# A kernel for a two-layer decoder trunk: in the second layer the weights' low part is made by ScalarE and an accumulating DMA instead of VectorE

## The chip, the core and the metric

The kernel runs on one core of one Trainium2 chip. TensorE (PE in the profile) multiplies and transposes, VectorE (DVE), ScalarE (ACT) and GpSimd (POOL) work on tiles in the on-chip memory, and SyncE (SP) issues the transfers from the device's memory. Every engine works through its own list of instructions in order; semaphores hold an instruction back until what it reads is there. The metric is the device time of one execution in microseconds (us), the median of several runs; lower is better.

## What is computed

The input is 512 positions of 1024 features in float32, the output has the same shape. There are two layers, each `x <- LayerNorm(alpha * x + sublayer(x))`.

The first (even) layer has two head groups, retention and a recurrent branch, which share one input projection and one output projection. The second (odd) layer is differential attention:

```
proj = einsum('bsd,de->bse', x, w_in);  q, k, v, g = split(proj)
q = rope(q) * d**-0.5;  k = rope(k)                        # 16 maps of 128 features
s = where(causal, q @ k^T, -inf);  p = softmax(s)          # two maps a head
w = p[:, :, 0] - lam * p[:, :, 1];  out = w @ v            # 8 heads of 256 features
out = out * rsqrt(mean(out**2) + eps) * subln_g * (1 - lambda_init) * silu(g)
y = out @ w_out
```

The input projection of the second layer is a 1024 x 8192 matrix, its output projection a 2048 x 1024 one. Everything is float32.

## The kernel before, in words

**Products.** To keep float32 precision, each operand is kept as two tiles of the matmul's own float32 format: a high part `h`, which is the value rounded by a cast, and a low part `l`, which is the value minus the high part. `mm3` (L148 to L151) adds three products for each product wanted: high by high, high by low, low by high.

**Weights.** A weight matrix comes in pieces of 128 x 1024 (512 KB). `order` lists them in the order of use: pieces 0 to 63 belong to the first layer, 64 to 143 to the second. 64 of the second layer's 80 pieces come from its input projection (`in_od_w`, no scale); the other 16 come from its output projection (`in_od_wo`) and are scaled while they are split. `fetch` (L163) takes the next piece: SP loads it into one of two raw buffers `w_r` (L171), and `split` (L139) makes the two parts: ScalarE casts `w_r` into `w<n>h` (L145), then VectorE writes `w_r` minus `w<n>h` into `w<n>l` (L146). A piece with a scale goes by L142 and L143. There are five buffers for split pieces (`wsp`), so the cast of piece n waits until TensorE has used piece n-5. For pieces 64 and 65, two further buffers are there (`wx`).

**Units of work.** The input projection is done in units. A `t_unit` takes one piece and gives 128 rows of q or k for all positions; an `s_unit` takes four pieces and gives v or g for four blocks of 128 positions (`sb`); an `out_unit` takes four pieces of the output projection. `take(ahead)` hands out the next piece and has written the fetches of `ahead` further pieces by then. Since TensorE's and SP's instructions stand in program order, this says where the loads stand on SP; the order on the other three engines comes from a list scheduler, which places an instruction by its own estimate of when everything is ready, with the priorities that the code gives (`tc.high_priority`).

**The order on TensorE** is written out: between the products of a unit, `side.tick()` starts steps of the other work (heads of attention, transposes after the LayerNorm) at counted places.

**From the first layer to the second.** The last `out_unit` of the first layer (`eo`) gives for each `sb` two banks of sums. VectorE adds them to `y` (L239), takes statistics (L334, L336), and normalises in two steps: L340, and after GpSimd has made the reciprocal root `lrs` (L325, L326) L342. TensorE transposes the result (`ht`, L561), ScalarE and VectorE split it into `hh` and `hl`. Then the first `s_unit` (`ov0`, pieces 64 to 67) starts.

**One block of attention** (a head, 128 positions; 32 blocks): TensorE scores `as`, VectorE the row minimum (L591), ScalarE the exponentials `e` (L594), VectorE the difference of the two maps (L602), TensorE transposes (`wt`, L606), ScalarE and VectorE split, TensorE multiplies by v into the bank `po`, of which there is one. Then ScalarE sums squares (L621), GpSimd makes the reciprocal root `ars` (`rs_t` L325, `ars` L326), VectorE multiplies (`o`, L625), TensorE transposes `o` back into `po` (L630), ScalarE and VectorE split it into `om<hd>h` and `om<hd>l`. Only then can the next block use the bank.

Of the kernel before, what the change touches and what calls it, by code (L numbers as in the profile page):

```python
# [8 lines left out]
F32 = mybir.dt.float32  # L9
F32R = mybir.dt.float32r  # L10
AF = mybir.ActivationFunctionType
ALU = mybir.AluOpType
# [83 lines left out]
def trunk(ctx: ExitStack, tc: tile.TileContext, a):  # L96
    nc = tc.nc
# [21 lines left out]
    ALL = slice(None)  # L119
# [7 lines left out]
    def bank(pl, tag, name):  # L127
        return pl.tile([P, 512], F32, tag=tag, name=name)

    def pair(pl, shape, tag, name, **kw):  # L130
        return tuple(pl.tile(shape, F32R, tag=tag + x, name=name + x, **kw) for x in "hl")
# [4 lines left out]
    def cut(t, *ix):  # L136
        return t[0][ix], t[1][ix]

    def split(src, dst, scale=None):  # L139
        if scale is not None:  # L140
            s = sg[:, scale:scale + 1]
            nc.scalar.activation(out=dst[0], in_=src, func=AF.Identity, scale=s)  # L142
            nc.vector.scalar_tensor_tensor(out=dst[1], in0=src, scalar=s, in1=dst[0].bitcast(F32), op0=ALU.mult, op1=ALU.subtract)  # L143
            return
        nc.scalar.copy(out=dst[0], in_=src)  # L145
        nc.vector.tensor_tensor(out=dst[1], in0=src, in1=dst[0].bitcast(F32), op=ALU.subtract)  # L146

    def mm3(out, l, r, start, stop):  # L148
        nc.tensor.matmul(out=out, lhsT=l[0], rhs=r[0], start=start, stop=False)  # L149
        nc.tensor.matmul(out=out, lhsT=l[0], rhs=r[1], start=False, stop=False)  # L150
        nc.tensor.matmul(out=out, lhsT=l[1], rhs=r[0], start=False, stop=stop)  # L151

    def load(name, shape, src, pl=None, tag=None, bufs=None):
        t = (pl or const).tile(shape, F32, tag=tag or name, name=name, bufs=bufs)
        nc.sync.dma_start(out=t, in_=src)
        return t
# [3 lines left out]
    order, ready = [], []  # L160
    extra, stats = {}, {}

    def fetch(parts=((0, D),)):  # L163
        if len(ready) < len(order):
            n = len(ready)
            src, scale = order[n]
            raw = wraw.tile([P, D], F32, tag="raw", name=f"w{n}_r")
            w = pair(extra.pop(n, wsp), [P, D], "w", f"w{n}")
            for lo, hi in parts:
                c = slice(lo, hi)  # L170
                nc.sync.dma_start(out=raw[:, c], in_=src[:, c])  # L171
                split(raw[:, c], cut(w, ALL, c), scale=scale)
                yield
            ready.append(w)

    taken = [0]

    def take(ahead):
        taken[0] += 1
        while len(ready) < min(taken[0] + ahead, len(order)):  # L180
            list(fetch())
        return ready[taken[0] - 1]

    def t_unit(act, name):
        w = take(2)
        ps = bank(ps_pj, "pj", name + "_ps")
        for kt in range(KT):
            mm3(ps, cut(w, ALL, slice(kt * P, kt * P + P)), cut(act, ALL, kt), kt == 0, kt == KT - 1)
            side.tick()
        return ps  # L190
# [65 lines left out]
    for kind, i in ev:  # L256
        if kind in ("ro", "lo", "out"):
            order += [(eo[2 * i + j + n], None) for n in {"ro": (0,), "lo": (8,), "out": (8, 0)}[kind] for j in range(2)]
        else:
            n = 4 if kind == "v" else 1  # L260
            order += [(ew[ei + j], None) for j in range(n)]
            ei += n
    order += [(eo[n], None) for n in (14, 15, 6, 7)]
    od = [("v", 0), ("g", 0), ("qk", 0), ("qk", 1), ("qk", 2)]
    for g in range(1, 4):
        od += [("g", g), ("v", g), *[("o", (2 * g - 2, 2 * g - 1))] * (g < 3), ("qk", 2 * g + 1), *[("qk", 2 * g + 2)] * (g < 3)]
# [20 lines left out]
    x = pair(big, [P, KT, S], "x", "x")  # L287
    xr = big.tile([P, KT, S], F32, tag="y", name="xr")
    halves = fetch(((0, HALF), (HALF, D)))
    for n, (lo, hi) in enumerate(((0, 1), (1, 2), (2, 4), (4, 6), (6, 8))):  # L290
        nc.sync.dma_start(out=xr[:, lo:hi], in_=a["xt"][:, lo:hi])
        for kt in range(lo, hi):
            split(xr[:, kt], cut(x, ALL, kt))
        if n < 2:
            next(halves)
            if n == 1:
                list(halves)
        elif n < 4:
            list(fetch())
# [217 lines left out]
    for kind, i in ev:  # L517
        if kind == "v":
            if i:
                for j in range(4):  # L520
                    side.need(job["ret", j], lambda: j in seen)
            v = v_even(i)
        elif kind == "xb":
            if i % 2 == 0:
                raw = load(f"gw{i}", [P, 4 * P], a["gw"][i // 2], pl=es, tag="es")
                gw[0] = pair(two, [P, 4 * P], "gw", f"gw{i}", bufs=1)
                split(raw, gw[0])
            job["lru", i] = side.add(lru(i, t_unit(x, f"xb{i}"), mixes(("lru", i // 2))), "lru", 2)
        elif kind == "q":
            dec[i] = load(f"dec{i}", [P, S], a["dec"][i], pl=two, tag="dec")  # L530
            q[i] = rope(t_unit(x, f"q{i}"), "q", f"q{i}")
        elif kind == "k":
            job["ret", i] = side.add(retention(i, q.pop(i), rope(t_unit(x, f"k{i}"), "k", f"k{i}"), v, dec.pop(i), mixes(("ret", i // 2))), "ret", 1, RET_START[i])
        elif kind in ("ro", "lo", "out"):
            even_out({"ro": ("ret",), "lo": ("lru",), "out": ("lru", "ret")}[kind], i, f"{kind}{i}")
        else:
            ps = t_unit(x, f"{kind}{i}")
            if len(users) >= 5:
                side.need(job[users[-5]])
            users.append(("ret" if kind == "gr" else "lru", i))  # L540
            g = gp.tile([P, S], F32, tag="g", name=f"{kind}{i}")
            silu(ps, g, f"{kind}{i}")
            gates[kind, i] = g
        if (kind, i) == ("gr", 1):
            for sb in range(SB):
                nc.sync.dma_start(out=y[:, sb], in_=a["x"][sb])
# [227 lines left out]
```

## Time and profile before

| | |
|---|---|
| median of 3 runs | 944.74 us (944.48 to 944.75) |
| the profiled execution | 944.8 us, its span in the profile 943.0 us |
| busy share of the span | PE 98%, DVE 73%, ACT 49%, POOL 6% |
| granted TensorE clock | 0.997 |
| transfers | 88.94 MB, 94 GB/s over the span, all issued by SP |
| the second layer's matmuls | begin at 409.6 us |

How to read it: a row of the timeline gives the start in us from the span's start, the duration in us, the engine, the line of the kernel, the operation, `out<-in` by the program's names, and in brackets the engine's idle time before it and what released it. Buffer numbers are left out in most names, but pieces and heads keep theirs (`w85h` is the high part of piece 85). The names `w00h` to `w73h` with two digits that stand beside `po` are not pieces but the transposed attention weights of a head and block. Matmuls overlap: their durations are longer than the distance between their starts, so starts are what counts.

### The profile page before, as it was taken

To read this page: it belongs to the slowest core of one execution; us is meant where nothing else is said; L and a number is where in the kernel's file an instruction comes from. 1 tells how busy PE (TensorE), PEld (TensorE's weight loads), DVE (VectorE), ACT (ScalarE), POOL (GpSimd) and SP (SyncE) were. 2 spreads that over 40 slices of the span, in tenths; PEclk is the share of its full clock that TensorE was granted. 3 is DMA by queue.
4 is the path that set the end of the run, shared out by engine and by line. 5 is a ranking of instruction groups with operands and counts; after the bars stand their busy time and mean duration, and the time that the engine had idled before them with its cause. 6 is when DMAs were issued, how large, how long until landed. Compare 5 with 4: busy or idle time off the path is not lost.

```text
span 943.0 us, 11558 instructions
## 1 busy us (share of the span) xinstructions
PE 924.9 (98%) x4327; PEld 764.4 (81%) x4327; DVE 692.8 (73%) x1171; ACT 462.7 (49%) x749; POOL 55.7 (6%) x117
## 2 busy tenths in 40 slices
PE   9999999999999999999999999999999999999995
PEld 7888888878887888888887888888788888887884
DVE  5877997878779988994489854478744488536687
ACT  5567786566474776423334454233453234444230
POOL 0000000000000000000001210100100001101012
PEclk9999999999999999999999999999999999999998
DMA  6562221512314123314221222042222142223102
GB/s 224 169 222 68 86 75 53 167 57 93 120 52 149 57 90 119 119 27 164 96 88 63 70 88 90 23 134 90 68 72 85 48 132 67 87 79 116 55 23 90
DMA packets 27416, 88.94 MB, mean 94 GB/s; under 512 B 3424, under 2 KB 3552, under 8 KB 27360
## 3 DMA queue, kind: packets, MB, share of 16 engines
q1 hardware_dynamic: 27360, 88.20, 28.1%
q8 instruction: 34, 0.56, 0.2%
q14 instruction: 22, 0.18, 0.1%
HBM read 86.09 MB, written 2.10 MB: 94 GB/s over the span
## 4 chain that ended last, share of the span: by engine, by line
PE 73%; DVE 13%; ACT 5%; issue 4%; DMA 2%; POOL 2%; SPq 0%; POOLq 0%; DVEq 0%; ACTq 0%
PE ov_ps L149 3%; PE ov_ps L150 3%; PE ov_ps L151 3%; PE og_ps L149 3%; PE og_ps L150 3%; PE og_ps L151 3%; PE oo_ps L149 2%; PE oo_ps L150 2%; PE oo_ps L151 2%; DMA w_r<-in_ev_w 2%; PE xb_ps L151 1%; PE xb_ps L149 1%; PE xb_ps L150 1%; PE gl_ps L149 1%; PE gl_ps L151 1%
## 5 line engine op out<-in xcount | busy, mean ns | idle before, releaser
L594 ACT ACTIVATE e<-as,nm 128x128 f32<-128x128 f32 (+3 forms) x64 | 33.2, 523 | 29.2 <-DVE nm L591 28.8
L625 DVE SCALAR_TENSOR_TENSOR o<-po,ars,og 128x256 f32<-128x256 f32 x32 | 15.5, 483 | 40.0 <-POOL ars L326 40.0
L591 DVE CUSTOM_DVE_ANT_0 as<-as,mask 128x128 f32<-128x128 f32 (+3 forms) x64 | 30.1, 509 | 1.9 <-PE as L151 1.9
L601 POOL TENSOR_SCALAR zr<-z 128x1 f32<-128x1 f32 x32 | 11.3, 352 | 308.9 <-ACT e L594 308.9
L325 POOL TENSOR_SCALAR rs_t<-bmv 128x1 f32<-128x1 f32 x8 | 3.8, 470 | 429.2 <-DVE bmv L336 429.2
L621 ACT ACTIVATE po<-po 128x256 f32<-128x256 f32 x32 | 11.9, 371 | 29.9 <-PE po L151 29.8
L325 POOL TENSOR_SCALAR rs_t<-ss,zr 128x1 f32<-128x1 f32 x32 | 15.9, 496 | 140.8 <-ACT po L621 135.8
L239 DVE TENSOR_TENSOR y<-oo_ps,y 128x512 f32<-128x512 f32 x24 | 16.2, 683 | 4.2 <-PE oo_ps L151 4.2
L326 POOL TENSOR_TENSOR ars<-rs_t,nhalf 128x1 f32<-128x1 f32 x32 | 18.9, 590 | 2.7
L466 DVE SCALAR_TENSOR_TENSOR xc<-xbp,vecs,xc 128x509 f32<-128x509 f32 (+2 forms) x24 | 17.8, 743 | 1.5 <-ACT xc L463 1.3
L602 DVE SCALAR_TENSOR_TENSOR e<-e,zr,e 128x128 f32<-128x128 f32 (+3 forms) x32 | 17.6, 551 | 1.0
L599 DVE RECIPROCAL zr<-z 128x1 f32<-128x1 f32 x32 | 5.2, 162 | 15.1 <-ACT e L594 14.9
L423 DVE TENSOR_TENSOR rsd<-rs,dec 128x512 f32<-128x512 f32 (+3 forms) x32 | 15.4, 483 | 0.9 <-PE rs L151 0.7
L630 PEld LDWEIGHTS po<-ident,o 128*128 128x128 f32 x64 | 8.3, 140 | 7.7 <-DVE o L625 4.5
L630 PE MATMUL po<-ident,o 128*128 128x128 f32 x64 | 12.6, 278 | 1.4 <-DVE o L625 1.3
L606 PE MATMUL wt<-ident,e 128*128 128x128 f32 x80 | 14.0, 273 | 0.0
L606 PEld LDWEIGHTS wt<-ident,e 128*128 128x128 f32 x80 | 10.4, 140 | 3.9 <-DVE e L602 0.4
L145 ACT CAST hh<-ht 128x512 fp32r<-128x512 f32 x8 | 4.7, 588 | 17.4 <-PE ht L561 17.4
L482 DVE TENSOR_TENSOR xbp<-xbp,xc 128x512 f32<-128x512 f32 x8 | 5.5, 690 | 10.0 <-ACT xbp L479 10.0
L594 ACT ACTIVATION_READ_ACCUMULATOR e<-as,nm 128x1 f32 x64 | 12.5, 196 | 0.0
L488 DVE SCALAR_TENSOR_TENSOR xc<-t,r 128x512 f32<-128x512 f32 x8 | 5.5, 691 | 9.0 <-ACT r L487 9.0
L342 DVE SCALAR_TENSOR_TENSOR y<-y,lrs,ln 128x512 f32<-128x512 f32 x16 | 11.3, 746 | 0.9 <-POOL lrs L326 0.9
(2665 smaller groups left out, 3411.2 us busy)
## 6 DMA issues: line engine op xcount, KB each, us to landing
w_r<-in_od_w SPq DMA_DIRECT2D x64, 512.0 KB, 3.3
w_r<-in_ev_w SPq DMA_DIRECT2D x47, 512.0 KB, 3.3
w_r<-in_ev_wo SPq DMA_DIRECT2D x16, 512.0 KB, 3.4
w_r<-in_od_wo SPq DMA_DIRECT2D x16, 512.0 KB, 3.3
dec<-in_dec SPq DMA_DIRECT2D x8, 256.0 KB, 3.8
y<-in_x SPq DMA_DIRECT2D x4, 512.0 KB, 6.8
out_h<-y SPq DMA_DIRECT2D x8, 256.0 KB, 2.1
xr<-in_xt SPq DMA_DIRECT2D x3, 512.0 KB, 7.1
```

The lines of the kernel that those rows point to most:

```text
L149: nc.tensor.matmul(out=out, lhsT=l[0], rhs=r[0], start=start, stop=False)
L150: nc.tensor.matmul(out=out, lhsT=l[0], rhs=r[1], start=False, stop=False)
L151: nc.tensor.matmul(out=out, lhsT=l[1], rhs=r[0], start=False, stop=stop)
L239: nc.vector.tensor_tensor(out=yy, in0=ps, in1=yy, op=ALU.add)
L325: nc.gpsimd.tensor_scalar(out=t, in0=var, scalar1=scale, scalar2=eps, op0=ALU.mult, op1=ALU.add)
L326: nc.gpsimd.tensor_tensor(out=out, in0=t, in1=nhalf[:, :1], op=ALU.pow)
L466: nc.vector.scalar_tensor_tensor(out=xc[:, sh:], in0=xb[:, :S - sh], scalar=conv_w(w, c), in1=xc[:, sh:], op0=ALU.mult, op1=ALU.add)
L591: nc.vector.tensor_tensor_reduce(out=ps[:, :n], in0=ps[:, :n], in1=mask[:, S - n:], scale=-QK_SCALE, scalar=3.0e38, op0=ALU.add, op1=ALU.m ...
L594: nc.scalar.activation(out=e, in_=ps[:, :n], func=AF.Exp, scale=-1.0, bias=nm, accum_out=z[:, mp:mp + 1])
L602: nc.vector.scalar_tensor_tensor(out=ee[0], in0=ee[1], scalar=zr[:, 0:1], in1=ee[0], op0=ALU.mult, op1=ALU.add)
L606: nc.tensor.transpose(out=pt[:, kb * P:kb * P + P], in_=ee[0][:, kb * P:kb * P + P], identity=ident)
L630: nc.tensor.transpose(out=pm[:, i * P:i * P + P], in_=o[:, i * P:i * P + P], identity=ident)
```

## The change

In the second layer, the pieces without a scale are made in another way: ScalarE casts the high part as before, ScalarE then writes minus the high part into the low part's tile, and GpSimd issues a DMA that reads the same 512 KB from the device's memory again and adds it to that tile. VectorE has no part in it. For `t_unit`s whose piece is one of the second layer's, `take` goes three pieces ahead instead of two.

```
+    second = len(order)          # after the first layer's pieces: 64
...
                 nc.sync.dma_start(out=raw[:, c], in_=src[:, c])
-                split(raw[:, c], cut(w, ALL, c), scale=scale)
+                if n >= second and scale is None:
+
+                    nc.scalar.copy(out=w[0][:, c], in_=raw[:, c])
+                    nc.scalar.activation(out=w[1][:, c], in_=w[0][:, c].bitcast(F32), func=AF.Identity, scale=-1.0)
+                    nc.gpsimd.dma_start(out=w[1][:, c], in_=src[:, c], accum_op=ALU.add)
+                else:
+                    split(raw[:, c], cut(w, ALL, c), scale=scale)
...
     def t_unit(act, name):
-        w = take(2)
+        w = take(3 if taken[0] >= second else 2)
```

In the changed program the line numbers from 172 on are 6 or 7 higher. TensorE's and SP's lists are the same but for buffer numbers. VectorE loses 64 instructions, ScalarE gains 64, GpSimd gains 64 DMA issues. The scheduler sets the order on these three engines anew. Three places matter for the prediction.

VectorE, at the passage from the first layer to the second, in the program before. `eo_ps_3419` and `eo_ps_3420` are the sums of the second block of positions, `eo_ps_3460` is the first half of the third block; the two rows L342 finish the first block:

```order
L336 BN_AGGR bmv<-bst 128x2
L340 SCALAR_TENSOR_TENSOR y<-y,bmv,ln_3350 128x512
L146 TENSOR_TENSOR w66l<-w_r,w66h 128x1024
L340 SCALAR_TENSOR_TENSOR y<-y,bmv,ln_3352 128x512
L342 SCALAR_TENSOR_TENSOR y<-y,lrs,ln_3354 128x512
L342 SCALAR_TENSOR_TENSOR y<-y,lrs,ln_3356 128x512
L239 TENSOR_TENSOR y<-eo_ps_3420,y 128x512
L239 TENSOR_TENSOR y<-eo_ps_3419,y 128x512
L334 BN_STATS bst<-y 128x6 x2
L239 TENSOR_TENSOR y<-eo_ps_3460,y 128x512
```

The same place in the changed program (L245 is the old L239, L341 the old L334, L347 and L349 the old L340 and L342):

```order
L343 BN_AGGR bmv<-bst 128x2
L347 SCALAR_TENSOR_TENSOR y<-y,bmv,ln_3350 128x512
L347 SCALAR_TENSOR_TENSOR y<-y,bmv,ln_3352 128x512
L245 TENSOR_TENSOR y<-eo_ps_3460,y 128x512
L341 BN_STATS bst<-y 128x6
L349 SCALAR_TENSOR_TENSOR y<-y,lrs,ln_3354 128x512
L349 SCALAR_TENSOR_TENSOR y<-y,lrs,ln_3356 128x512
L349 SCALAR_TENSOR_TENSOR y<-y,lrs,ln_3354 128x512
L349 SCALAR_TENSOR_TENSOR y<-y,lrs,ln_3356 128x512
L146 TENSOR_TENSOR hl<-ht_3483,hh 128x4x128
```

The first three rows are the second block's; the first two L349 rows, which finish the first block, now stand behind the addition of `eo_ps_3460` from the third block and its statistics.

ScalarE, in the first group of attention, the program before (`po_4414` is the third block's bank, `e_4398` the exponentials):

```order
L594 ACTIVATE e_4398,z<-as_4392,nm 128x512
L145 CAST w85h<-w_r 128x1024
L621 ACTIVATE po_4414,ss<-po_4414 128x256
L145 CAST q20oh<-q20o_c 128x512
L145 CAST om0h<-po_4414 128x2x128
```

The changed program:

```order
L601 ACTIVATE e_4424,z<-as_4418,nm 128x512
L174 CAST w85h<-w_r 128x1024
L175 ACTIVATE w85l<-w85h 128x1024
L628 ACTIVATE po_4440,ss<-po_4440 128x256
L145 CAST q20oh<-q20o_c 128x512
L145 CAST om0h<-po_4440 128x2x128
```

The writing of minus the high part (L175) has come between the cast of a piece and the sum of squares of an attention block. The same stands at pieces 86, 96, 109, 110, 116, 129 and 130; at piece 91 it stands behind the cast and ahead of two table loads and the next exponentials.

GpSimd, at the same place in the changed program (before, only the rows without DMA are there, in this order):

```order
L176 DMA w84l<-in_od_w 128x1024
L608 TENSOR_SCALAR zr<-z 128x1
L176 DMA w85l<-in_od_w 128x1024
L332 TENSOR_SCALAR rs_t<-ss,zr 128x1
L333 TENSOR_TENSOR ars<-rs_t,nhalf 128x1
```

The issue of the DMA for piece 85, which waits for ScalarE's L175, stands ahead of the two steps of the reciprocal root.

## The prediction

> **What bounds the kernel now.** I read the page's busy times first, then the table by stage, then TensorE's waits in the second layer.
>
> ```profile
> span 943.0 us, 11558 instructions
> PE 924.9 (98%) x4327; PEld 764.4 (81%) x4327; DVE 692.8 (73%) x1171; ACT 462.7 (49%) x749; POOL 55.7 (6%) x117
> ```
>
> TensorE works for 98% of the span. The second layer, from its first product to the start of its last output unit, is one row of the table by stage (time, then busy us of PE, PEld, DVE, ACT and POOL, granted clock, share of the DMA engines, GB/s):
>
> ```profile
> 409.60:907.90 498.30, 494.10 (x2391) 409.47 (x2390) 329.75 (x605) 201.76 (x399) 44.88 (x95) 1.00 0.26 83
> ```
>
> The change removes work from an engine that is 66% busy there (329.75 of 498.30). TensorE stays the bound, with the same list, so what can be won is TensorE's waiting on VectorE. In the same stage:
>
> ```profile
> PE po L630 <- DVE o L625: 1.3, 3, 0.5
> PE po L149 <- DVE om6l L146: 1.1, 3, 0.6
> PE po L149 <- DVE om0l L146: 0.7, 1, 0.7
> PE po L149 <- DVE om4l L146: 0.5, 2, 0.3
> PE po L149 <- DVE om2l L146: 0.5, 2, 0.3
> ```
>
> That is 4.1 us in all (1.3 + 1.1 + 0.7 + 0.5 + 0.5), and none of it is a wait for a piece. The question is therefore less what VectorE gains than which of the attention's steps, on ScalarE and GpSimd, come later.
>
> **The change part by part.**
>
> *Totals.* VectorE loses 64 subtractions like the one at 676.44 below (1.22 us), 78 us. ScalarE gains 64 writes of minus the high part. The cast takes 1.04 to 1.05 us for the same 1024 columns, the scaled write of an output piece 1.16; I take 1.1, so 70 us. ScalarE in the second layer goes from 202 to some 270 of 498 us. These totals are hidden beside TensorE; what counts is where each piece stands.
>
> GpSimd's DMA is new, and the trace has no transfer issued there. How long an issue holds GpSimd, D, lies between the 0.33 us in which SP issues the same transfer and the 3.3 us (median) that such a transfer takes to land, if GpSimd were held until then. I take 1.0, the middle of the two in ratio. How long the data takes after it, L, is at least the 3.1 us minimum of a plain load; a crowded plain load took 7.8, and two reads of that kind would be 15.6. I take 5.0, between one and two passes of 3.3.
>
> ```profile
> L171 SPq DMA_DIRECT2D w_r<-in_od_w x64: 327/328/1354, 377.7 to 835.9; - x64
> DMA to landing us min/median/max: 3.1/3.3/7.8
> 567.88 1.16 ACT L142 ACTIVATE w92h<-w_r,sg 128x1024 fp32r<-128x1024 f32 x1
> ```
>
> *The LayerNorm between the layers: +1.5.* In the changed order the rows that finish the first block of positions stand behind the sum and statistics of `eo_ps_3460`. Its last product:
>
> ```profile
> 399.36 1.41 DVE L342 SCALAR_TENSOR_TENSOR y<-y,lrs,ln 128x512 f32<-128x512 f32 x2
> 400.69 1.28 DVE L239 TENSOR_TENSOR y<-eo_ps,y 128x512 f32<-128x512 f32 x2
> 401.88 1.27 DVE L334 BATCH_NORM_STATS2 bst<-y 128x6 f32<-128x512 f32 x2
> ...
> 396.47 1.05 ACT L145 CAST w66h<-w_r 128x1024 fp32r<-128x1024 f32 x1 [2.96 <-DMA w_r<-in_od_w]
> ...
> 400.85 0.39 PE L151 MATMUL eo_ps<-w63h,retm3l 128*128 128x512 f32 x1
> ...
> 401.76 0.60 PE L561 MATMUL ht<-ident,y 128*128 128x128 f32 x4
> ```
>
> Before, VectorE finished the first half at 400.07 (399.36 + 0.7), 1.7 us ahead of the transposes at 401.76. Now it can begin the sum only at 401.3 (400.85 + 0.39), then 0.6 for the sum, 0.6 for the statistics, 0.7 for the first half: 403.2. TensorE waits there about 1.5 us, where it did not wait at all. GpSimd's `lrs` stands behind the issue for piece 66, which ScalarE has ready at 398.6 (396.47 + 1.05 + 1.1): with D = 1.0 it ends at 400.2, with 3.3 at 402.5, still in time, so GpSimd is not the price here.
>
> *The sum of squares behind piece 85: +1.1.* The third block of attention before:
>
> ```profile
> 513.49 1.04 ACT L145 CAST w85h<-w_r 128x1024 fp32r<-128x1024 f32 x1
> 514.42 0.38 ACT L621 ACTIVATE po<-po 128x256 f32<-128x256 f32 x1
> ...
> 515.02 0.27 POOL L325 TENSOR_SCALAR rs_t<-ss,zr 128x1 f32<-128x1 f32 x1 [1.58 <-ACT po L621]
> 515.37 0.55 POOL L326 TENSOR_TENSOR ars<-rs_t,nhalf 128x1 f32<-128x1 f32 x1
> ...
> 516.43 0.47 DVE L625 SCALAR_TENSOR_TENSOR o<-po,ars,og 128x256 f32<-128x256 f32 x1
> ...
> 516.96 0.44 PE L630 MATMUL po<-ident,o 128*128 128x128 f32 x2
> ```
>
> The reader is to see a chain with no slack: `o` ends at 516.90, the transposes follow at 516.96. Now ScalarE writes minus the high part until 515.6, GpSimd issues the DMA until 516.6, only then `rs_t`, `ars` 0.9 later at 517.5, `o` until 518.0: +1.1. With D = 0.33 the sum of squares decides (`rs_t` at 516.1): +0.6. With 3.3: +3.3.
>
> *The same behind pieces 109 and 129: +0.7 each.*
>
> ```profile
> 676.06 0.38 ACT L621 ACTIVATE po<-po 128x256 f32<-128x256 f32 x1
> ...
> 676.66 1.13 POOL L325 TENSOR_SCALAR rs_t<-ss,zr 128x1 f32<-128x1 f32 x1 [1.65 <-ACT po L621]
> 677.87 0.55 POOL L326 TENSOR_TENSOR ars<-rs_t,nhalf 128x1 f32<-128x1 f32 x1
> ...
> 676.44 1.22 DVE L146 TENSOR_TENSOR w109l<-w_r,w109h 128x1024 fp32r<-128x1024 f32 x1
> 678.46 0.48 DVE L625 SCALAR_TENSOR_TENSOR o<-po,ars,og 128x256 f32<-128x256 f32 x1 [0.80 <-POOL ars L326]
> ...
> 678.99 0.44 PE L630 MATMUL po<-ident,o 128*128 128x128 f32 x2 [0.46 <-DVE o L625]
> ```
>
> Here `rs_t` took 1.13 us instead of 0.27, beside VectorE's subtraction, which the change removes. So this place wins 0.86 and loses more: the sum of squares moves to 677.15, the DMA's issue ends at 678.25, `ars` at 679.15, `o` at 679.65, transposes at 679.7. With D = 0.33: +0.15; with 3.3: +3.0. Piece 129 stands in the same pattern. The Trainium skill, page "SBUF — State Buffer", section "Who interferes with whom", says that a VectorE instruction with two inputs in that memory contends with a GpSimd instruction that reads it; the lengthened row agrees (1.13 beside it, 0.27 without). By that rule the 0.86 us comes back, as counted; without it each of the two places would cost 1.6, and the sum would be 1.7 us higher.
>
> *Behind pieces 96 and 116: +0.1 each.*
>
> ```profile
> 589.67 1.05 ACT L145 CAST w96h<-w_r 128x1024 fp32r<-128x1024 f32 x1
> 591.48 0.63 POOL L325 TENSOR_SCALAR rs_t<-ss,zr 128x1 f32<-128x1 f32 x1 [20.10 <-ACT po L621]
> 594.13 0.38 PE L630 MATMUL po<-ident,o 128*128 128x128 f32 x2
> ```
>
> ScalarE is through at 591.8, GpSimd at 592.8, `o` 1.4 later at 594.2 (0.9 and 0.48), against 594.13. With D = 3.3: +2.4; with 0.33 nothing.
>
> *The exponentials behind piece 91: +0.7.*
>
> ```profile
> 559.03 1.05 ACT L145 CAST w91h<-w_r 128x1024 fp32r<-128x1024 f32 x1 [0.16 <-PE og_ps L151]
> 564.56 0.20 ACT L594 ACTIVATION_READ_ACCUMULATOR e<-as,nm 128x1 f32 x1
> 565.30 0.49 DVE L602 SCALAR_TENSOR_TENSOR e<-e,zr,e 128x256 f32<-128x256 f32 x1
> 566.22 0.38 PE L606 MATMUL wt<-ident,e 128*128 128x128 f32 x2
> ```
>
> ScalarE has no gap from the cast to the exponentials, so 1.1 us more there ends `e` on VectorE at 566.9 instead of 565.8, and the transposes at 566.22 wait 0.7.
>
> *What is won: -0.5.* `om0l` was late (0.7 us) because the subtraction of piece 83 stood ahead of it on VectorE; most of that wait goes. The waits for `om6l`, `om4l` and `om2l` lie beside output pieces, which stay as they were.
>
> *Do the pieces come in time?* Two tight places. Behind the LayerNorm, the cast of piece 67 waits for a buffer; behind an output unit, that of piece 97 (and 117 likewise).
>
> ```profile
> 405.61 1.06 ACT L145 CAST w67h<-w_r 128x1024 fp32r<-128x1024 f32 x1 [1.50 <-PE eo_ps L151]
> 409.04 0.39 PE L151 MATMUL eo_ps<-w63h,retm3l 128*128 128x512 f32 x1
> 614.82 1.05 ACT L145 CAST w97h<-w_r 128x1024 fp32r<-128x1024 f32 x1 [2.91 <-PE oo_ps L151]
> 624.18 0.39 PE L151 MATMUL q31o_ps<-hh,w97l 128*128 128x512 f32 x1
> ```
>
> Piece 97: cast, a small step, minus the high part until 617.2, D to 618.2, L to 623.2, wanted at 624.18: hidden, with 1 us left. Piece 67: all is 1.5 later with the wait above; cast and minus until 409.3, D and L to 415.3. It is wanted 5 us after the row at 409.04, so at 415.6: hidden by 0.3 us. If that cover is gone, each us of D + L over 6.3 costs one here, over 7.0 one at each of the other two places. The other pieces have more room, by the five buffers. The DMA engines are 26% busy, so a second transfer of each piece, even at three times a plain load's work, stays under 100% (0.26 + 3 x 0.21).
>
> *The sum* is 1.5 + 1.1 + 1.4 + 0.2 + 0.7 - 0.5 = +4.4 us on the profiled execution's 944.8 (0.06 over the median): **949.2 us**. With D = 0.33 it is +2.55, so 947.4; with D = 3.3 it is 1.5 + 3.3 + 6.0 + 4.8 + 0.7 - 0.5 = +15.8, so 960.6.
>
> **The rivals.**
>
> *The added data comes too late.* If L is 7.8, the highest plain landing, piece 67 costs 2.5 and pieces 97 and 117 1.8 each: 949.2 + 6.1 = 955.3. At 15.6 it would be 979. For it: the transfer reads two operands. Against it: the transfers of this stage land in 3.3 at the median. It decides from D + L = 6.3 on.
>
> *GpSimd is held by its issues.* D near 3.3 gives 960.6. For it: GpSimd's steps are already stretched beside VectorE. Against it: SP's issue takes a tenth of that. The Trainium skill, "SBUF — State Buffer", section "A bandwidth-pool intuition that's wrong (but worth ruling out)", has a GpSimd-issued DMA at about 620 ns alone and about 3100 beside a VectorE copy. Taken as estimates of D, these give 947.9 and 959.4; no run here shows such a DMA yet.
>
> *Not slower: the relief of VectorE decides.* If GpSimd's issue takes next to nothing and ScalarE's extra write falls into its gaps, the waits for `o` (1.3) and `om0l` (0.7) go and nothing comes: 942.8. For it: VectorE's subtractions do stretch GpSimd's steps, and the released raw buffer lets loads start 1.2 us earlier. Against it: the LayerNorm's 1.5 us and piece 91's 0.7 hang on no unknown price, only on the order of rows.
>
> **How the numbers follow.** The forecast has a chance of 0.48, with its own range 946.7 to 953; late data 0.17; a held GpSimd 0.10; not slower 0.25, of which half would be under 942.9. A measurement of this kernel tells 0.2% (1.9 us) from no change. Slower: 0.48 + 0.17 + 0.10 = 0.75; within 0.2%: 0.13; faster: 0.12. The range of 944 to 960 leaves out the best of the last case and the tails of late data and held issues.
>
> **What would show it.** In the changed kernel's profile: `ht` at the first block waits for VectorE's L349, about 1.5 us; transposes of `o` wait at pieces 85, 109 and 129, with GpSimd's `ars` as VectorE's releaser; `wt` waits 0.7 at piece 91; VectorE's busy time is 78 us lower, ScalarE's 70 higher. GpSimd's issue and the landing time of its 64 DMAs are to be read directly. Wrong would be waits of TensorE for a `w<n>l` by a DMA (late data), GpSimd rows more than 2 us apart around each issue (held), or no wait at `ht`.

## The result

The changed kernel takes **952.14 us** (median of 4 runs, 951.89 to 952.67) against 944.75 us before (944.48 to 944.80): 1.0079 times as long, 95% interval 1.0066 to 1.0091. It is slower by 7.4 us; the prediction was 949.2 us, so +4.4, with a range of 944 to 960.

The page of the changed kernel, its span, its engines and its two transfer queues (packets, MB, time of the packets as a share of 16 engines' span):

```profile
span 950.4 us, 11715 instructions
PE 925.3 (97%) x4327; PEld 764.4 (80%) x4327; DVE 623.3 (66%) x1107; ACT 528.4 (56%) x813; POOL 107.4 (11%) x181
q1 hardware_dynamic: 27360, 88.20, 27.6%
q0 software_dynamic: 9216, 33.56, 20.2%
```

TensorE's busy time is what it was (925.3 against 924.9) and the span is 7.4 us longer, so all of it is waiting. VectorE lost 69.5 us, ScalarE gained 65.7, GpSimd gained 51.7: the work went where the change sends it. The prediction had 78 and 70: it multiplied whole rows by 64, while neighbouring rows of one engine overlap by about 0.1 us. These totals have no part in its sum. The new queue is q0: 33.56 MB took 20.2% of the transfer engines' time, the plain loads' 88.20 MB 27.6%. Per byte that is 1.9 times as much.

TensorE's waits in the changed kernel (what waited, for whom, us in total, times, longest), those that are new or have grown:

```profile
PE po L637 <- DVE o L632: 5.5, 5, 1.7
PE ht L568 <- DVE y L349: 1.5, 1, 1.5
PE q51o_ps L151 <- DMA w117l<-in_od_w: 0.8, 1, 0.8
PE q31o_ps L151 <- DMA w97l<-in_od_w: 0.7, 1, 0.7
PE wt L613 <- DVE e L609: 0.5, 1, 0.5
```

The wait for `o` was 1.3 us and is 5.5; the other four rows did not exist. The row for `om0l` (0.7) is gone.

This view shows waits that can be put down to a releaser. To compare places, I also took from the trace, for every matmul, the distance to the start of the next one, less the distance that back-to-back matmuls of its size have (227 ns for 512 columns, 116 for 256, 70 for 128), and summed what lies over 60 ns. From 376 us on, this *lost time* is 14.9 us before and 22.4 us after; the 7.5 between them agrees with the 7.4 us by which the span grew. By place, in us:

| step | predicted | measured |
|---|---|---|
| LayerNorm between the layers | +1.5 | +1.6 |
| sum of squares behind piece 85 | +1.1 | +1.7 |
| behind pieces 109 and 129 | +1.4 | +2.1 |
| behind pieces 96 and 116 | +0.2 | +1.1 |
| exponentials behind piece 91 | +0.7 | +0.8 |
| data of pieces 97 and 117 | 0 | +2.1 |
| won at `om0l`, at `o` and beside them | -0.5 | -2.3 |
| sum | +4.4 | +7.1 |

The remaining 0.4 us is spread over distances that changed by less than 0.1 us each.

**The LayerNorm.** VectorE and TensorE after the change, the timeline at the place where the first block of positions is finished:

```profile
401.34 0.69 DVE L245 TENSOR_TENSOR y<-eo_ps,y 128x512 f32<-128x512 f32 x1 [0.96 <-PE eo_ps L151]
402.06 0.69 DVE L341 BATCH_NORM_STATS2 bst<-y 128x6 f32<-128x512 f32 x1
402.67 2.72 DVE L349 SCALAR_TENSOR_TENSOR y<-y,lrs,ln 128x512 f32<-128x512 f32 x4
...
403.46 0.66 PE L568 MATMUL ht<-ident,y 128*128 128x128 f32 x4 [1.49 <-DVE y L349]
```

VectorE sat idle for 0.96 us until the third block's product was there, though the first block's L349, whose `lrs` was ready at 400.12, stood behind it. Sum, statistics and the first half follow as worked out; TensorE waits 1.49.

**Piece 85.** ScalarE, GpSimd, VectorE and TensorE after the change, the timeline of the third block of attention:

```profile
514.44 1.06 ACT L175 ACTIVATE w85l<-w85h 128x1024 fp32r<-128x1024 f32 x1
515.41 0.36 ACT L628 ACTIVATE po<-po 128x256 f32<-128x256 f32 x1
...
515.91 0.89 POOL L176 DMA_DIRECT2D w85l<-in_od_w  x1 [2.75 <-ACT po L628]
516.91 0.59 POOL L332 TENSOR_SCALAR rs_t<-ss,zr 128x1 f32<-128x1 f32 x1
517.58 0.56 POOL L333 TENSOR_TENSOR ars<-rs_t,nhalf 128x1 f32<-128x1 f32 x1
...
518.71 0.44 PE L637 MATMUL po<-ident,o 128*128 128x128 f32 x2 [1.73 <-DVE o L632]
```

The issue holds GpSimd for 0.89 us, close to the 1.0 taken. But it starts 0.41 us after ScalarE's write ends (515.50 to 515.91), and `rs_t` starts 0.11 us behind it. From ScalarE's end to `rs_t` it is 1.4 us, not 1.0.

**Pieces 97 and 117.** The timeline at piece 117, the time of that piece's transfer from its issue to its landing, and the table by stage around it (time, then busy us of PE, PEld, DVE, ACT and POOL, granted clock, share of the transfer engines, GB/s; the share adds up the packets' times and can pass 1.00), all after the change:

```profile
751.98 1.06 ACT L175 ACTIVATE w117l<-w117h 128x1024 fp32r<-128x1024 f32 x1
...
753.46 0.95 POOL L176 DMA_DIRECT2D w117l<-in_od_w  x1 [4.60 <-ACT w117l L175]
...
761.07 0.50 PE L151 MATMUL q51o_ps<-hh,w117l 128*128 128x512 f32 x1 [0.80 <-DMA w117l<-in_od_w]
```

```profile
DMA to landing us min/median/max: 7.6/7.6/7.6
```

```profile
742.00:750.00 8.00, 8.00 (x45) 6.83 (x45) 3.26 (x6) 1.44 (x4) 0.81 (x2) 1.00 0.01 2
754.00:758.00 4.00, 4.00 (x19) 3.34 (x18) 0.69 (x1) 3.17 (x3) 1.42 (x3) 1.00 0.87 206
758.00:762.00 4.00, 3.20 (x15) 2.33 (x14) 2.08 (x4) 1.08 (x2) 0.71 (x1) 1.00 1.07 248
```

The transfer engines stand idle while the output unit runs (share 0.01), and then loads and added transfers come together (0.87, 1.07). In that crowd the data takes 7.6 us from the issue; over all 64 transfers the time is

```profile
DMA to landing us min/median/max: 5.3/5.9/10.2
```

### The profile page after: what moved, and what is told of

Same layout as the page of the kernel before. It is cut to its first block, busy times and chain, and to the rows that moved or that the text cites. A ratio compares the mean times of both kernels' runs of the same rounds, so it can differ in the third digit from the quotient of the medians.

```text
span 950.4 us, 11715 instructions
## 1 busy us (share of the span) xinstructions
PE 925.3 (97%) x4327; PEld 764.4 (80%) x4327; DVE 623.3 (66%) x1107; ACT 528.4 (56%) x813; POOL 107.4 (11%) x181
## 3 DMA queue, kind: packets, MB, share of 16 engines
q1 hardware_dynamic: 27360, 88.20, 27.6%
q0 software_dynamic: 9216, 33.56, 20.2%
## 4 chain that ended last, share of the span: by engine, by line
PE 70%; DVE 12%; ACT 7%; issue 5%; DMA 4%; POOL 2%; SPq 0%; POOLq 0%; DVEq 0%; ACTq 0%
PE ov_ps L151 3%; PE ov_ps L150 3%; PE ov_ps L149 3%; PE og_ps L149 2%; PE og_ps L150 2%; PE og_ps L151 2%; PE oo_ps L149 2%; PE oo_ps L150 2%; PE oo_ps L151 2%; DMA w_r<-in_ev_w 2%; PE xb_ps L151 1%; PE xb_ps L149 1%; PE xb_ps L150 1%; ACT e L601 1%; PE gl_ps L149 1%
## 5 line engine op out<-in xcount | busy, mean ns | idle before, releaser
L245 DVE TENSOR_TENSOR y<-oo_ps,y 128x512 f32<-128x512 f32 x24 | 16.3, 684 | 5.0 <-PE oo_ps L151 5.0
L609 DVE SCALAR_TENSOR_TENSOR e<-e,zr,e 128x128 f32<-128x128 f32 (+3 forms) x32 | 17.6, 551 | 1.0
L332 POOL TENSOR_SCALAR rs_t<-ss,zr 128x1 f32<-128x1 f32 x32 | 9.8, 307 | 70.2 <-ACT po L628 68.5
L349 DVE SCALAR_TENSOR_TENSOR y<-y,lrs,ln 128x512 f32<-128x512 f32 x16 | 11.2, 747 | 1.8 <-POOL lrs L333 1.8
```

Source lines behind the costliest of these rows:

```text
L245: nc.vector.tensor_tensor(out=yy, in0=ps, in1=yy, op=ALU.add)
L609: nc.vector.scalar_tensor_tensor(out=ee[0], in0=ee[1], scalar=zr[:, 0:1], in1=ee[0], op0=ALU.mult, op1=ALU.add)
```

## The experiments

Each kernel was timed beside the kernel before on the same chip. Pieces "as before" are cast on ScalarE and subtracted on VectorE; the others are made the new way. The lost time is that of the profiled execution, whose own time stands beside it.

| kernel | median, us | ratio to before (95%) | profiled execution | lost time from 376 us on |
|---|---|---|---|---|
| before | 944.24 to 944.75 | | 944.8 | 14.9 |
| the change | 952.14 | 1.0079 (1.0066 to 1.0091) | 952.26 | 22.4 |
| 64 to 67 as before | 952.94 | 1.0086 (1.0071 to 1.0101) | 951.46 | 22.4 |
| 64 to 71 as before | 953.50 | 1.0096 (1.0082 to 1.0110) | 953.13 | 23.3 |
| 85, 96, 109, 116, 129 as before | 947.48 | 1.0028 (1.0017 to 1.0040) | 947.49 | 17.7 |
| 97, 117 as before | 949.48 | 1.0050 (1.0035 to 1.0065) | 949.26 | 20.2 |
| minus on ScalarE, sum on VectorE | 949.08 | 1.0047 (1.0032 to 1.0062) | 948.94 | 19.6 |
| before, with idle GpSimd transfers | 946.70 | 1.0021 (1.0011 to 1.0030) | 947.46 | 17.6 |
| all twelve as before | 946.80 | 1.0015 (1.0005 to 1.0024) | 947.41 | 16.9 |
| the change, two pieces ahead | 952.05 | 1.0078 (1.0063 to 1.0093) | 952.12 | 22.4 |
| before, three pieces ahead | 944.85 | 1.0000 (0.9991 to 1.0010) | 944.87 | 15.0 |
| nineteen as before | 941.87 | 0.9972 (0.9962 to 0.9983) | 942.50 | 12.1 |
| only 83 the new way | 944.15 | 0.9997 (0.9988 to 1.0006) | 944.09 | 14.3 |
| nineteen as before, sum on VectorE | 944.90 | 1.0008 (0.9999 to 1.0017) | 944.68 | 15.0 |

### The LayerNorm: pieces 64 to 67 as before

```diff
-                if n >= second and scale is None:
+                if n >= second + 4 and scale is None:
```

> Undone for pieces 64 to 67 alone: they are split by VectorE as before, so the rows that finish the first block of positions stand ahead of the next block's sums again. Theory (the places add up): the wait of 1.5 us at ht goes and nothing else changes, 952.1 - 1.5 = 950.6 us; the five waits for o and the two for pieces 97 and 117 stay as in the changed kernel. Rival (the time comes from the second reading of the pieces in general, the wait at ht only moves the same time): 952 us, with another wait grown in its place.

Measured: 952.94 us (951.46 to 954.26 in 4 runs), no gain. The profiled execution is the fastest of the four. In it the wait at `ht` is gone, as the theory has it, but another came. TensorE's wait for piece 68 and the time of that piece's transfer:

```profile
PE og_ps L150 <- DMA w68l<-in_od_w: 1.4, 1, 1.4
...
DMA to landing us min/median/max: 7.7/7.7/7.7
```

In the changed kernel piece 68's data took 5.4 us and nobody waited. Here the issue for piece 69 followed it 2.0 us later instead of 4.3 (428.95 behind 426.95, against 430.71 behind 426.42), and the two transfers and the loads shared the engines for longer. That the crowd made the data late is argued from this, not shown. What is shown is that one wait took the other's place: the first new piece was wanted earlier once TensorE no longer waited at the LayerNorm, and its data took longer. Two of the four executions lie 2 us and more above the profiled one (953.84 and 954.26), with a mean granted clock of 0.994 and 0.995 where the other two have 0.997 and 0.998. That fits a stretch of lower clock behind the same wait, as the run with all twelve costly pieces shows it below, but neither of the two was profiled.

### The sums of squares: pieces 85, 96, 109, 116 and 129 as before

```diff
-                if n >= second and scale is None:
+                if n >= second and scale is None and n not in (85, 96, 109, 116, 129):
```

> Undone for pieces 85, 96, 109, 116 and 129 alone, the five behind which TensorE waited for o. Theory: the waits for o fall from 5.5 us to about 1.0 (0.45 each stay at 109 and 129, where VectorE's subtraction stretches GpSimd's step again), so 952.1 - 4.5 = 947.6 us. Rival (GpSimd is late because of all its issues, not of the one just ahead): waits for o stay above 3 us, 950.5 us or more.

Measured: 947.48 us, as the theory has it (4.7 us less than the change). The wait for `o` in this run, and its longest:

```profile
PE po L637 <- DVE o L632: 1.7, 3, 0.9
```

5.5 became 1.7, of which 0.9 is a new wait: the block behind piece 86, which comes earlier now, meets ScalarE's write and GpSimd's issue for that piece. Lost time fell by 5.2 us at the five places (1.9 at piece 85, 1.1 each at 109 and 129, 0.55 each at 96 and 116), and 1.0 came back at the neighbour.

### The late data: pieces 97 and 117 as before

```diff
-                if n >= second and scale is None:
+                if n >= second and scale is None and n not in (97, 117):
```

> Undone for pieces 97 and 117 alone, whose added data came 0.8 us too late. Theory: both waits go and pieces 98 and 118 still come in time, since they have some 3 us more: 952.1 - 1.5 = 950.6 us. Rival (the transfers are short of rate behind an output unit, so the next piece is late instead): 951.5 us or more, with a wait for piece 98 and 118.

Measured: 949.48 us, 2.7 us less than the change, where 1.5 was expected. Both waits are gone and no other piece became late. The lost time at these places fell by 2.1 us (0.9 and 1.0 at the two first uses, 0.1 each at the matmul behind), more than the 1.5 that the view of waits shows; most of the rest lies before 60 us, where the first weights are awaited and where the lost time differs by up to 1 us between any two profiles.

### Where the price lies: ScalarE or GpSimd

Two kernels each do one half. In the first, ScalarE writes minus the high part and VectorE adds the raw piece:

```diff
-                    nc.gpsimd.dma_start(out=w[1][:, c], in_=src[:, c], accum_op=ALU.add)
+                    nc.vector.tensor_tensor(out=w[1][:, c], in0=raw[:, c], in1=w[1][:, c].bitcast(F32), op=ALU.add)
```

> ScalarE writes minus the high part for all 64 pieces as in the changed kernel, but VectorE adds the raw piece to it; GpSimd issues no DMA. Theory (ScalarE's write and GpSimd's issue are in series ahead of the reciprocal root, each some 1 us): no wait at ht, waits for o at 109 and 129 of about 1.4 us each, since the sum of squares is 1.0 later, and 0.6 to 1.0 at 85, 0.6 at the exponentials behind 91: 947.5 to 949.5 us. Rival (GpSimd's issue is the whole price): 944.5 to 945.5 us.

Measured: 949.08 us, as the theory has it. In the second, the kernel before keeps its subtraction, and GpSimd issues a small transfer behind each cast, whose data nobody reads:

```diff
                 nc.sync.dma_start(out=raw[:, c], in_=src[:, c])
                 split(raw[:, c], cut(w, ALL, c), scale=scale)
+                if n >= 64 and scale is None:
+                    extra_t = scr.tile([P, P // 2], F32R, tag="scr", name=f"scr{n}")
+                    nc.gpsimd.dma_start(out=extra_t, in_=w[0][:, :P // 2])
```

> The kernel before, with one GpSimd DMA more for each of the 64 pieces: it copies 64 columns of the high part to a tile that nobody reads, so GpSimd pays an issue for 128 rows behind each cast, without ScalarE's extra write and almost without data. Theory (in series, and partly beside other waits): at 85 the issue ends at about 515.9, so o is 0.5 later; at 109 and 129 it lies beside VectorE's subtraction that stretches the step anyway, 0 to 0.2 each; 945 to 946.5 us. Rival (GpSimd's issue is the whole price): the waits for o near 5.5 us, 948.5 us or more.

Measured: 946.70 us. TensorE's waits, first with ScalarE's half, then with GpSimd's:

```profile
PE po L637 <- DVE o L632: 3.8, 4, 1.3
```

```profile
PE po L634 <- DVE o L629: 1.8, 4, 0.5
PE ht L565 <- DVE y L346: 1.7, 1, 1.7
```

ScalarE's row makes most of the waiting for `o` (3.8, against 1.3 before and 5.5 after), and no wait at `ht`. With GpSimd's issues alone there is one, though VectorE still has all its subtractions. VectorE's rows at that place in this run (L243 adds the sums, L344 is the first step of normalising, L346 finishes the block):

```profile
399.45 1.28 DVE L243 TENSOR_TENSOR y<-eo_ps,y 128x512 f32<-128x512 f32 x2
...
402.20 0.75 DVE L344 SCALAR_TENSOR_TENSOR y<-y,bmv,ln 128x512 f32<-128x512 f32 x1
402.87 1.41 DVE L346 SCALAR_TENSOR_TENSOR y<-y,lrs,ln 128x512 f32<-128x512 f32 x2
```

The first block is finished only at 402.87, behind the second block's sums and its first step of normalising, although its `lrs` was ready at 399.30. So the scheduler's order makes this wait too, but it is another order than in the changed kernel, where VectorE sat idle for the third block's product. That GpSimd's issues are enough to move these rows is shown; what part the lost subtractions have in the changed kernel's order is not. This expectation had not counted that wait; without it the run agrees (+0.5 at piece 85, under 0.1 at pieces 109 and 129). The run prices GpSimd's half too low: its small transfers are issued in 0.53 to 0.73 us against 0.85 to 1.06 in the changed kernel, and right behind the cast, without ScalarE's second row ahead of them.

How the two halves add up at piece 109 is to be seen in GpSimd's rows, first with VectorE's addition (its row on VectorE last), then in the changed kernel:

```profile
679.60 0.89 POOL L332 TENSOR_SCALAR rs_t<-ss,zr 128x1 f32<-128x1 f32 x1 [2.74 <-ACT po L628]
680.57 0.55 POOL L333 TENSOR_TENSOR ars<-rs_t,nhalf 128x1 f32<-128x1 f32 x1
...
679.13 1.23 DVE L176 TENSOR_TENSOR w109l<-w_r,w109l 128x1024 fp32r<-128x1024 f32 x1 [0.77 <-ACT w109l L175]
```

```profile
681.49 0.90 POOL L176 DMA_DIRECT2D w109l<-in_od_w  x1 [2.74 <-ACT po L628]
682.50 0.25 POOL L332 TENSOR_SCALAR rs_t<-ss,zr 128x1 f32<-128x1 f32 x1
682.84 0.56 POOL L333 TENSOR_TENSOR ars<-rs_t,nhalf 128x1 f32<-128x1 f32 x1
```

`rs_t` takes 0.89 us beside VectorE's addition and 0.25 without it. That pays for most of the issue's 1.0: lost time at this place is 0.6 before, 1.5 with the addition, 1.7 with the transfer. The Trainium skill, "SBUF — State Buffer", section "Who interferes with whom", has a VectorE instruction with two inputs in that memory contend with a GpSimd instruction that reads it; these rows agree.

### All twelve costly pieces as before

```diff
-                if n >= second and scale is None:
+                if n >= second + 4 and scale is None and n not in (85, 91, 96, 97, 109, 116, 117, 129):
```

> The changed kernel with pieces 64 to 67, 85, 91, 96, 97, 109, 116, 117 and 129 split as before, the other 52 in the new way. Theory: all the places of the loss are gone and the gain stays (the wait for om0l, 0.7, and for o behind piece 83, 0.4): 943.4 to 944.2 us, slightly under the kernel before. Rival (the 52 other pieces have a price of their own): 946 us or more.

Measured: 946.80 us (944.55 to 947.41 in 10 runs), slower than before, so the theory fell. Piece 68 is late again, by 1.9 us, and the 0.9 behind piece 86 is there. A third loss was not in any theory. TensorE and the table by stage around piece 68's first use:

```profile
436.30 0.50 PE L150 MATMUL og_ps<-w68l,hh 128*128 128x512 f32 x1 [1.94 <-DMA w68l<-in_od_w]
```

```profile
435.00:436.00 1.00, 0.00 (x0) 0.00 (x0) 0.00 (x0) 0.00 (x0) 0.00 (x0) 1.00 1.06 246
...
437.00:438.00 1.00, 1.00 (x5) 0.75 (x4) 0.00 (x0) 0.97 (x2) 0.00 (x0) 0.53 1.02 270
438.00:439.00 1.00, 1.00 (x4) 0.81 (x3) 0.22 (x1) 0.75 (x2) 0.37 (x1) 0.50 1.10 283
439.00:440.00 1.00, 1.00 (x4) 0.81 (x3) 0.47 (x1) 0.00 (x0) 0.52 (x1) 0.50 1.08 229
440.00:441.00 1.00, 1.00 (x5) 0.72 (x5) 0.00 (x0) 0.85 (x1) 0.00 (x0) 0.76 1.02 209
```

Behind the wait the granted clock was 0.5 for some 3.4 us; the matmuls of that stretch lost 1.7 us more. So this wait cost 3.8 us (2.1 and 1.7). Four of the ten runs lie at 944.55 to 945.44 and six at 946.48 to 947.41; that the four are those without the slow stretch fits the 2 us between them and the mean granted clocks (0.996 to 0.998 in the four, 0.994 to 0.996 in the six), but only one of the ten, the slowest, was profiled.

### The look-ahead

The other part of the change, alone and left out:

```diff
-        w = take(3 if taken[0] >= second else 2)
+        w = take(2)
```

> The changed kernel with two pieces ahead again instead of three. Theory: the five buffers set the lead, the order of rows hardly moves: 952.1 us within 0.3. Rival (the third piece ahead covers the longer way of a piece): waits for pieces by DMA grow, 954 us or more.

```diff
-        w = take(2)
+        w = take(3 if taken[0] >= second else 2)
```

> The kernel before with three pieces ahead in the second layer, all else as it was. Theory: 944.7 us within 0.3. Rival (going ahead by three shifts rows on ScalarE and VectorE and is part of the loss): 946 us or more.

Measured: 952.05 and 944.85 us. It does nothing in either kernel.

### Nineteen pieces as before, and one piece alone

```diff
-                if n >= second and scale is None:
+                if n >= second + 8 and scale is None and n not in (85, 86, 91, 96, 97, 109, 110, 116, 117, 129, 130):
```

> Of the changed kernel, pieces 64 to 71, 85, 86, 91, 96, 97, 109, 110, 116, 117, 129 and 130 are split as before; the other 45 are made the new way. Theory (what is lost comes from single pieces that stand ahead of a group norm or the layer norm or land late, and the two waits for VectorE behind pieces 83 and 84 are the only gain): the waits of the run with twelve pieces undone, piece 68's data 1.9 us and the gated row behind piece 86 0.9 us, go as well, the om0l wait of 0.7 and the gated row's 0.4 stay away: 943.5 to 944.4 against 944.7 before. Rival (whichever piece is the first new one behind undone ones finds its data late, as piece 68 did): a DMA wait of 1 us or more at piece 72 or another, and 945.5 to 947.

Measured: **941.87 us**, 0.9972 times the time before (0.9962 to 0.9983): faster than both kernels, and more so than expected. The two longest of TensorE's waits that are left in the second layer; `om2l` and `om4l` are as before:

```profile
PE po L149 <- DVE om6l L146: 1.1, 3, 0.6
PE po L637 <- DVE o L632: 0.7, 2, 0.4
```

No wait for data, none for `om0l`, and `o` is down from 1.3 to 0.7. Lost time against before: -0.9 ahead of `om0l`, -0.5 behind piece 83, -0.2 each in the blocks at pieces 104 and 124 (the subtractions ahead of them are those of pieces 107 and 127), 0.1 to 0.2 at some more transposes: -2.8 in all.

With only piece 83 made the new way, the piece whose subtraction stood ahead of `om0l`:

```diff
-                if n >= second and scale is None:
+                if n == 83:
```

> Only piece 83 is made the new way; its row on VectorE (1.23 us) stood right ahead of om0l, for which TensorE waited 0.7 us. Theory (that wait is what the change gained): the wait is gone, nothing else moves, 943.8 to 944.3 against 944.7 before. Rival (the work behind takes it back, since the next group norm's rows come no earlier): 944.5 to 945.0, with the 0.7 us in the gated row's wait at the next group.

Measured: 944.15 us against 944.32, a difference inside the interval. In the profile the place ahead of `om0l` still loses 0.3 us of its 0.9, and the next block but one loses 0.3 that it had not lost before. One piece is too little.

### The same nineteen, with the sum on VectorE

The kernel of 941.87 us with its transfer replaced, as in the first half-experiment, by VectorE's addition.

> The 45 pieces of the faster version, but VectorE adds the raw piece to minus the high part; no transfer by GpSimd. Theory (the faster version's gain over before is VectorE's relief at om0l, at the gated rows behind pieces 83, 104 and 124): the waits of before for om0l (0.7) and for the gated rows (1.3) are back, 944.3 to 945.0. Rival (the gain lies in another order of the rows, which ScalarE's second row brings too): 942 to 943.

Measured: 944.90 us. Its waits:

```profile
PE po L637 <- DVE o L632: 1.2, 3, 0.5
...
PE po L149 <- DVE om0l L146: 0.7, 1, 0.7
```

They are those of before (1.3 and 0.7). So what the faster version wins is VectorE's relief, and GpSimd's transfer is what brings it.

### The LayerNorm again: pieces 64 to 71 as before

```diff
-                if n >= second and scale is None:
+                if n >= second + 8 and scale is None:
```

> Of the changed kernel, pieces 64 to 71 are split as before; the other 56 are made the new way. When only 64 to 67 were undone, the layer norm's wait went and piece 68's data came 1.4 us late. Theory (piece 68 was late because it was the first new piece while the loads crowded; piece 72 has five buffers of time in hand): neither wait shows, so 952.1 - 1.5 = 950.6 or a little less (950.0 to 950.9). Rival (the first new piece is late wherever it stands): a wait of 1 us or more for piece 72's data, 951.6 to 953.

Measured: 953.50 us (952.59 to 953.97). In the profile neither the wait at `ht` nor one at pieces 68 to 72 shows, as the theory has it, but the time is worse: piece 117's data, some 320 us further on, took 1.0 us longer than in the changed kernel, and behind that wait the clock fell again. The wait and two slices of the table by stage:

```profile
PE q51o_ps L151 <- DMA w117l<-in_od_w: 1.8, 1, 1.8
```

```profile
762.00:763.00 1.00, 1.00 (x4) 0.71 (x4) 0.00 (x0) 0.41 (x1) 0.19 (x1) 0.50 1.10 266
763.00:764.00 1.00, 1.00 (x4) 0.81 (x3) 0.00 (x0) 0.00 (x0) 0.67 (x1) 0.50 1.04 209
```

The data took 8.6 us from its issue instead of 7.6. Why the loads stood closer together there is open. Both theories on the time were wrong; what holds is that the LayerNorm's 1.6 us goes when the first pieces are made as before, and that the late pieces can take it back.

## Why the prediction was right, and where it was not

**The sign and the main reason held.** The prediction asked which of the attention's steps come later instead of what VectorE gains, and that question gave the right places: `ht` for L349, the transposes of `o` at 85, 109 and 129, `wt` behind piece 91 are all in TensorE's waits. Undoing five pieces gave back 4.7 of 7.4 us.

**The LayerNorm: exact** (1.5 predicted, 1.49 waited). It came from the order of rows and known durations alone. What in the change sets that order was not asked: the run with idle transfers shows that GpSimd's issues alone can move these rows, though to another place.

**Piece 91: right** (0.7 against 0.8 of lost time, of which the view of waits shows 0.5). **Piece 67: right.** "Hidden by 0.3 us": its data landed at 415.3, the time that the prediction gave, and TensorE did not wait.

**D was right as the issue's own length and too small as a step.** The issue takes 0.85 to 1.06 us, close to the 1.0 taken. The prediction let GpSimd issue at the moment ScalarE ends and `rs_t` follow at once. The trace has 0.41 us ahead of the issue and 0.11 behind it, 1.4 us in all. That is +0.4 at each of the five places (at 96 and 116 the prediction had 0.1, since everything just fitted). At 85, `rs_t` was also 0.59 long instead of the 0.27 that was carried over. At 109 and 129, the time that `rs_t` won (1.13 to 0.25) was as counted. These places together were mis-sized by 2.2 us (4.9 against 2.7).

**L was right for an idle queue and wrong for a crowded one.** "Hidden, with 1 us left" at pieces 97 and 117 was the step that failed. D and L were taken as 6.0; from ScalarE's end to the landing it took 8.0 at piece 117 (753.04 to 761.0, with the 0.42 ahead of the issue and 7.6 from it). The rival on late data named these two places, the point from which it decides (7.0) and the price (one us for each us over it): 1.0 each, as measured. The prediction had dismissed it by the median load of the stage and by a mean share ("the DMA engines are 26% busy"). The table by stage shows a share of 1.00 where it counts. The same stretch, before and after:

```profile
620.00:640.00 20.00, 20.00 (x90) 16.57 (x89) 15.79 (x20) 7.12 (x8) 0.00 (x0) 1.00 0.44 142
```

```profile
620.00:640.00 20.00, 19.25 (x85) 15.65 (x84) 7.51 (x12) 11.83 (x13) 4.58 (x6) 1.00 1.00 249
```

**The gain was mis-sized** (-0.5 against -2.3). The prediction counted the one named wait, `om0l`, and cut it; it left out the wait for `o` behind piece 83 and the two small ones at pieces 104 and 124, which also stood behind subtractions.

**The rivals.** GpSimd held by its issue for 3 us did not happen: no issue is over 1.07 us, also beside VectorE's instructions with two inputs. (With D = 3.1 the prediction's own terms give 959.6, not 959.4.) Of the two figures that the page of the Trainium skill has ("SBUF — State Buffer", "A bandwidth-pool intuition that's wrong (but worth ruling out)"), the 620 ns alone is not met as an issue's length (0.86 to 0.93 where VectorE does nothing beside it); the 3100 ns beside a VectorE copy is not tested, since no VectorE copy stands beside an issue in the changed kernel's trace. The case "not slower" was wrong for the change as it is, but its mechanism is real: it is the 2.8 us of lost time that the version with nineteen pieces as before wins.

The sum came out 2.9 us under the time because two terms were too small by 4.3 (issue 2.2, late data 2.1) and one gain was too small by 1.8; the rest is small differences. That the two errors pull opposite ways is luck: with the gain as measured and all else as predicted, the sum would have been +2.6.

## What to carry to other kernels

A step that moves from a busy engine to idle ones is priced where it lands: look, for each moved row, at what stands right behind it on its new engine, and use it only for the pieces where nothing does. Whether a second transfer is hidden is read in the stretches where the loads come in bursts, not from a mean share. A wait that goes away hands its time requirement to the next piece in line, so an undo is tested together with its neighbours.

## What the runs showed of the hardware

- **A transfer that adds, issued by GpSimd,** holds GpSimd for 0.85 to 1.07 us per 512 KB piece and starts about 0.4 us behind the instruction it waits for. Its data lands 5.3 us after the issue's start where nothing else is moved (piece 67: the 99 GB/s of those 5.3 us are its own 512 KB), and up to 10.2 in a crowd (up to 11.2 in the run with all twelve as before). A plain load of the same size took 3.1 to 7.8 before.
- **A wait of TensorE of about 2 us can cost nearly as much again.** Behind waits in which the next matmul came 2.1 and 2.0 us late (piece 68 with twelve pieces as before, piece 117 with eight), the granted clock was 0.5 for some 3.4 us; behind one of 1.9 (piece 85 in the changed kernel) it stayed at 1.00. The Trainium skill, "TensorE: Matmul & The Clock Gate", section "Part 1: The HAM clock gate (the "warmup" mystery)", has the clock halve after an idle window of about 3.4 us and return after a busy one of that length. The slow stretch agrees in length; the idle time that was enough here was shorter, and what decides between 1.9 and 2.0 us isn't settled by these runs.
